# A decoder layer on one core: gate and up rows of the experts dealt to partitions in runs of eight

## The chip, the cores and the metric

The kernel runs on one core of one Trainium2 chip. The metric is device time in microseconds (us), from runs of the whole layer. Engines are named as in the profile: PE is the matmul engine (PEld its weight load), DVE the vector engine, ACT the scalar engine, POOL GpSimd, SP the engine that issues most of the transfers. The transfers of all queues run on 16 DMA engines.

## The reference, cut to what matters

One layer of a decoder with 1024 tokens of 1024 columns: a combined input projection, two kinds of causal attention side by side, an output projection, cross-attention into 256 memory tokens, and a mixture of 32 experts in 4 groups, of which each token takes the best two of its best group. The change is in the last part:

```python
hf = h.reshape(n_tok, d)                       # normalised rows, 1024 x 1024
xb = h_pad[tok]                                # the rows that chose expert e
hidden = jax.nn.silu(xb @ w_gate[e]) * (xb @ w_up[e])     # 1024 x 256 each
y = (hidden @ w_down[e]) * wt[:, None]                     # 256 x 1024
out = zeros.at[slot_token].add(y)
```

`xb @ w_gate[e]` sums over the 1024 columns of a row. In which order, and which 128 of them share a step, is free, as long as the columns of `xb` and the rows of the weights agree.

## The kernel before, in words

All instructions are recorded first, with the tiles that they read and write, and then issued in an order that a list scheduler with a fixed cost model finds (class `Sched`; what it issues has line 481 in the profile). Everything of size is one of 50 tiles of 4 KB per partition.

**Router.** For each tile of 128 tokens, `r_keep(t)` multiplies the rows with the norm's gain on POOL (`xn<-xr,gb`), scales them with each row's factor on ACT, and stores them with SP into the DRAM table `XN`, one row of 4 KB a token. On DVE run the choice of the experts (`r_top`, tiles `rtmp` and `A`), the ranks (`r_rank`) and the factors (`fs`). `r_index` makes the table of row numbers `gidx`, by which the experts gather.

**Experts.** `experts()` goes over the 32 experts. For each, `moe_piece` loads six pieces of 512 KB into tiles `eraw`: pieces 0 to 3 hold 256 rows each of gate and of up (two DMAs of 256 KB), pieces 4 and 5 hold 128 rows each of down (one DMA of 512 KB). `m_split` makes of each piece two parts that the matmul takes exactly: `ehi` (a copy on ACT) and `elo` (a subtraction on DVE). `m_x` gathers up to 96 token rows from `XN` (POOL, `xg<-XN,gidx`) and transposes them, 128 columns at a time, into `xT`. `m_gu` multiplies: for each of 8 blocks of 128 columns three matmuls (high by high, high by low, low by high) into one PSUM bank whose first 256 columns are gate and last 256 up. `m_h` and `m_d` transpose the product and multiply with down; POOL adds the rows into `ACC` with an indirect DMA. The first four experts multiply with the down weights as they are (`WHOLE_D`); no expert does so with gate and up (`WHOLE_GU` is empty).

In `moe_piece`, piece j of gate takes the weight rows 256j to 256j + 255; partition p gets rows 256j + p and 256j + 128 + p. So each partition gets two runs of 1 KB from gate and two from up. The transposed block k of a token row holds columns 128k to 128k + 127.

A last part (from line 1828 on) handles experts with more than 96 tokens, if there are any. In the profiled execution its body is not entered.

Of the kernel before, what the change touches and what calls it, by code (L numbers as in the profile page):

```python
# [22 lines left out]
P = 128  # L23
D = 1024
S = 1024
KT = D // P
# [53 lines left out]
# Instructions are recorded with the tiles they read and write, and issued in the order in which  # L80
# a list scheduler with a simple cost model starts them.
# [6 lines left out]
def _sizes(side, kw, shape=None):  # L88
    """The axes of one side of a rearrange pattern, as lists of names."""
    out, group = [], None  # L90
    for tok in side.replace("(", " ( ").replace(")", " ) ").split():
        if tok == "(":
            group = []
        elif tok == ")":
            out.append(group)
            group = None
        elif group is None:
            out.append([tok])
        else:
            group.append(tok)  # L100
    return out


class View:
    """A part of a lazily allocated tile."""
# [58 lines left out]
class LazyTile:  # L164
    def __init__(self, pool, shape, dtype, kw, slot):
        self.pool, self.shape, self.dtype, self.kw, self.slot = pool, tuple(shape), dtype, kw, slot
        self.real, self.log, self.left, self.end = None, [], 0, 0
        self.seq, self.strict, self.reserve = slot["count"], False, slot["reserve"]
        self.cap = pool.sched.caps.get(kw["name"])
        slot["count"] += 1  # L170
        # a PSUM bank is taken only once all that is to be written there by the tensor engine can be
        self.whole, self.wait, self.at = pool.psum and kw["name"] != "acc", 0, 0
# [29 lines left out]
class Sched:  # L202
    def __init__(self, nc):
        self.nc, self.ops = nc, []
        self.free = dict.fromkeys(("tensor", "vector", "scalar", "gpsimd", "sync"), 0)
        self.dma_free, self.table = 0, 0
        # for tiles of some names, the places that they share
        self.caps = {n: [0] * c for n, c in dict(CAPS, bank=NB_S, acc=NB_A, lbank=NB_L).items()}
        self.window, self.busy, self.warm = 0, 0, False
        for e in self.free:  # L210
            setattr(self, e, Engine(self, e))
# [7 lines left out]
    def cost(eng, name, a, k, out, views):  # L219
        """Nanoseconds on the engine, and until the result is there."""  # L220
# [27 lines left out]
    def either(self, *ways):  # L248
        """Records an instruction, or a few of one engine; several ways: the scheduler chooses one."""
# [22 lines left out]
        for v in views:  # L272
# [3 lines left out]
            # the tensor engine's writes to a bank stay in order  # L276
# [3 lines left out]
            for o, b, ow in t.log:  # L280
                # the engines take turns at a bank, whatever they do there
# [11 lines left out]
    @staticmethod  # L293
    def hold(*views):
        """Instructions recorded after the next flush use these tiles too."""
        for v in views:
            v.tile.left += 1
# [6 lines left out]
    def flush(self):  # L304
# [17 lines left out]
        queue = {e: [] for e in self.free}     # (time ready, idx, op)  # L322
        avail = {e: [] for e in self.free}     # (idx, op)
# [6 lines left out]
        while done < len(ops):  # L330
            best = None
            for e in self.free:
# [4 lines left out]
                # the first one whose tiles have room  # L337
# [55 lines left out]
    def seen(op, eng):  # L393
        """When an engine can go on from an instruction."""
# [6 lines left out]
    def room(self, op):  # L401
        """When the tiles that the instruction is the first to use can be had; None: not known yet."""
# [16 lines left out]
        for slot, n, before, reserve in need.values():  # L419
            # some places are for the tiles that come before in program order  # L420
# [38 lines left out]
    def clock(self, now, cost):  # L459
        """The tensor engine's clock is halved after a window in which it was little busy."""  # L460
# [55 lines left out]
def hybrid_kernel(ctx: ExitStack, tc: tile.TileContext, a, out):  # L516
# [28 lines left out]
    # everything of size is a tile of 4 KB per partition  # L545
# [8 lines left out]
    def carve(name):  # L554
        """Small tensors as parts of such a tile."""
# [77 lines left out]
    def rsqrt(dst, v, tmp):  # L633
        """dst = 1 / sqrt(v): a first guess from the bits, and three steps of Newton's."""
# [7 lines left out]
    def rsqrt_mean(dst, ss, n, tmp):  # L642
        """dst = 1 / sqrt(ss / n + eps); ss is lost."""
# [3 lines left out]
    def two(name):  # L647
        """Two parts of a [128, 512] operand."""
        return t4(name, P, 2, CH, dt=F32R)
# [13 lines left out]
    def split(dst, src, g=None, eng="vector"):  # L663
        """src (times g) as the sum of two parts that the tensor engine takes exactly."""
# [7 lines left out]
    class Weights:  # L672
        """Column blocks of weights, loaded ahead of their use, in parts [rows, 128 of them, columns]."""
# [16 lines left out]
        def get(self, i):  # L690
            """A function from the row block to its two parts."""
# [12 lines left out]
    def weave(*lists):  # L704
        """Calls the units of all lists, each list's spread evenly over all or a part of the time."""
# [8 lines left out]
    # =================== projections ===================  # L714
# [26 lines left out]
    def x_first(t):  # L741
        """The same for one tile, so that the first products need not wait for a chunk."""
# [20 lines left out]
    # low-rank queries, keys and the rotary key, token-major  # L763
# [22 lines left out]
    # angles of the rotary part  # L786
# [4 lines left out]
    def reduce_angle(ang, tmp):  # L791
        """ang modulo 2 pi, within [-pi, pi] but for rounding"""
# [10 lines left out]
    def c_angles():  # L803
# [6 lines left out]
        # feature-major tables: even heads' has the rotary rows last, odd heads' first; the other rows scale only  # L810
# [32 lines left out]
    def out_split(po, dsts, g=None):  # L843
        """Two parts of a PSUM bank, stored; dsts: where to, and from which partitions."""
# [5 lines left out]
    # rotary key, four copies side by side  # L850
# [25 lines left out]
    # differential queries and keys  # L876
# [15 lines left out]
    # latent queries: columns of a head as [no position | rotary | rotary, halves swapped],  # L892
    # odd heads with the first part last
# [39 lines left out]
    def v_out(po, n0, nh, dst, t):  # L933
        """Values of nh heads from n0 on as [high | low] (even heads) and [low | high]."""
# [36 lines left out]
    # =================== attention ===================  # L971
# [12 lines left out]
    def make_dist(i):  # L984
        """-|pos_q - pos_k| / scale, and far below zero above the diagonal"""
# [81 lines left out]
    def item(kind, h, c):  # L1067
        """Units of one head and half of its queries: the softmaxes, the products with the values."""
# [73 lines left out]
    def attention(items):  # L1142
        """All units of some items: an item's softmaxes along with the products of the one before."""
# [7 lines left out]
    # =================== output projection, memory, router ===================  # L1151
# [8 lines left out]
    # memory's keys and values  # L1160
# [47 lines left out]
    # output norms: one factor for each token and head  # L1208
# [70 lines left out]
    def factors(c, tiles, name):  # L1279
        """1 / rms of the rows of some tiles, in two steps."""  # L1280
# [10 lines left out]
    def cross_units(c):  # L1291
        """The rows of a chunk, transposed, times the gain and in two parts; their factors are for later."""
# [12 lines left out]
    # cross-attention  # L1305
# [78 lines left out]
    # router  # L1384
# [26 lines left out]
    def r_T(t, kk):  # L1411
        """Half a tile's columns, transposed and in two parts."""
# [19 lines left out]
    def r_keep(t):  # L1432
        """The tile's normalised rows, kept in DRAM for the experts."""
        x = t4("xn")
        nc.gpsimd.tensor_mul(x, xr[t], rt["gb"])
# [4 lines left out]
    def r_factors(c, *sizes):  # L1440
        """Units of the rows' factors, and of the tiles' transposes, logits and rows."""
# [16 lines left out]
    def first_max(v, m, oh, cm, wcol):  # L1458
        """One-hot of the first largest along the last axis, and the largest, step by step."""
# [16 lines left out]
    def r_top(c):  # L1476
        """The chunk's choices of experts."""
# [20 lines left out]
    def r_weights(c, take, gl, gm, goh, m12):  # L1498
# [15 lines left out]
        # in three exact parts  # L1514
# [13 lines left out]
    def r_rank(c):  # L1528
        """Rank of each choice among its expert's."""
# [25 lines left out]
    def r_index():  # L1555
        """The table of the first NS choices of every expert."""
# [15 lines left out]
    def r_slots():  # L1572
        """The weights of the table's choices."""
# [15 lines left out]
    def r_over():  # L1589
        """Blocks beyond an expert's first: how many, and where they start."""  # L1590
# [17 lines left out]
    # =================== experts ===================  # L1608
# [12 lines left out]
    def moe_piece(e, j):  # L1621
        """Of an expert's six pieces: two row blocks of gate and up each, or a row block of down."""
# [3 lines left out]
        if j < 4:  # L1626
            for w, o in ((w_g, 0), (w_u, 256)):
                nc.sync.dma_start(raw[:, :, o:o + 256], w[e, j * 256:(j + 1) * 256].rearrange("(k p) f -> p k f", p=P))
        else:
            nc.sync.dma_start(raw.rearrange("p a c -> p (a c)"), w_d[e, (j - 4) * P:(j - 3) * P])  # L1630

# [12 lines left out]
    def m_x(e):  # L1644
        """Gathers the expert's tokens and transposes them."""
# [19 lines left out]
    def m_gu(e):  # L1665
        gu = bank()
        for k in range(KT):
            x = st[e]["x"][k // 4]
            sl = slice((k % 4) * NS, (k % 4 + 1) * NS)
            if e in WHOLE_GU:  # L1670
                mm(gu[0:NS], x[:, sl], pieces[e, k // 2][:, k % 2], start=k == 0, stop=k == KT - 1)
            else:
                wh, wl = st[e][k // 2]
                mm3(gu[0:NS], x[:, 0, sl], x[:, 1, sl], wh[:, k % 2], wl[:, k % 2], k == 0, k == KT - 1)
# [52 lines left out]
    # =================== the order of it all ===================  # L1727
# [21 lines left out]
    # units of work on a common time line, which gives the priorities  # L1749
# [9 lines left out]
    def place(units, *knots):  # L1759
        """Spreads units over the stretches between knots, as many on each."""  # L1760
# [57 lines left out]
    # choices beyond an expert's first NS, in blocks of one expert each  # L1818
# [10 lines left out]
    with tc.If(rnov > 0):  # L1829
# [30 lines left out]
        # a choice that is among the first NS matches no lane  # L1860
# [40 lines left out]
        with tc.For_i(0, rnov, 1) as b:  # L1901
# [7 lines left out]
            for i in range(4):  # L1909
                for src, o in ((w_g, 0), (w_u, 256)):  # L1910
                    nc.sync.dma_start(wgu[i][:, :, o:o + 256], src[bass.ds(ev, 1), i * 256:(i + 1) * 256].rearrange(
                        "o (k p) f -> p (o k) f", p=P))
# [36 lines left out]
    # =================== end: sum and norm ===================  # L1949
# [40 lines left out]
```

## Time and profile before

| | |
|---|---|
| median of 3 runs | 1263.01 us (1262.37 to 1264.27) |
| the profiled execution, first to last instruction | 1263.7 us (no other time of that execution is given) |
| PE busy | 1119.0 us, 89% |
| DVE busy | 903.8 us, 72% |
| ACT busy | 803.1 us, 64% |
| POOL busy | 423.3 us, 33% |
| DMA packets | 177883, 256.56 MB, of them 131058 under 2 KB |

The page shows one execution. Its first part gives each engine's busy time, the second cuts the span into 40 slices of 31.6 us and gives the busy share of each engine and of the DMA engines in tenths. A busy share says where an engine works, not what ends the wait of another; for that there are the chain of waits (the work that ended last, followed back) and the list of who waited for whom. A DMA share over 100% in a short stretch means that an engine works on more than one packet at a time.

### The profile page before, as it was taken

How to read it: one execution, taken by the hardware profiler on the slowest of the kernel's cores; microseconds unless marked ns; L12 is line 12 of the kernel's file. 1: busy time of each engine (PE TensorE's matmuls, PEld its weight loads, DVE VectorE, ACT ScalarE, POOL GpSimd, SP SyncE). 2: the span in 40 equal slices, each digit the busy share in tenths (PEclk: the TensorE clock that was granted, in tenths of full speed). 3: DMA queues.
4: the chain of work that ended last, by engine and by line, in shares of the span. 5: the costliest groups of instructions: out<-in, count | busy, mean ns of one | idle time of the engine just before them, and what ended most of it. 6: DMA issues, size and time to landing. Idle time of an engine off the chain costs nothing.

```text
span 1263.7 us, 19612 instructions
## 1 busy us (share of the span) xinstructions
PE 1119.0 (89%) x6285; PEld 915.9 (72%) x6285; DVE 903.8 (72%) x2100; ACT 803.1 (64%) x1597; POOL 423.3 (33%) x370
## 2 busy tenths in 40 slices
PE   4999999998888998888999999995999988888970
PEld 3988888896767876677899888874666656566640
DVE  5846525478799889988573467786678877777855
ACT  5744326679786778777371455632677877777862
POOL 2214311278554555746411001233133322221110
PEclk8999999997898999788999999995999999999995
DMA  9039897359636462445531132766899999999977
GB/s 291 18 106 314 316 356 223 110 169 265 155 96 146 123 162 62 114 121 194 173 122 47 34 103 70 284 233 232 251 293 275 299 291 311 307 316 315 334 218 272
DMA packets 177883, 256.56 MB, mean 203 GB/s; under 512 B 17035, under 2 KB 131058, under 8 KB 177778
## 3 DMA queue, kind: packets, MB, share of 16 engines
q1 hardware_dynamic: 161728, 208.22, 53.0%
q0 software_dynamic: 15680, 46.75, 12.2%
q8 instruction: 50, 0.82, 0.3%
q14 instruction: 55, 0.45, 0.1%
q10 hardware_dynamic: 370, 0.32, 0.1%
HBM read 208.57 MB, written 55.05 MB: 209 GB/s over the span
## 4 chain that ended last, share of the span: by engine, by line
PE 49%; DMA 24%; DVE 15%; ACT 6%; issue 4%; POOL 1%; SPq 0%; ACTq 0%; DVEq 0%; POOLq 0%
PE lbank L481 29%; DMA eraw<-in_w_expert_up_dram 16%; PE bank L481 15%; PE acc L481 5%; DMA eraw<-in_w_expert_down_dram 4%; DVE mx L481 4%; DVE pT L481 1%; ACT pt L481 1%; DVE pt L481 1%; DMA eraw<-in_w_expert_gate_dram 1%; DVE ss L481 1%; ACT pT L481 1%; DMA ACC<-y,gidx 1%; DVE yt L481 1%; DVE wlo L481 1%
## 5 line engine op out<-in xcount | busy, mean ns | idle before, releaser
L481 DVE TENSOR_TENSOR elo<-eraw,ehi 128x1024 fp32r<-128x1024 f32 x184 | 221.6, 1222 | 54.5 <-ACT ehi L481 50.7
L481 ACT CAST ehi<-eraw 128x1024 fp32r<-128x1024 f32 x184 | 189.6, 1050 | 38.8 <-DMA eraw<-in_w_expert_up_dram 28.5
L481 PE MATMUL bank<-ehi,xT 128*96 128x512 f32 x512 | 175.3, 414 | 16.8 <-ACT y L481 15.6
L481 PE MATMUL bank<-k,q 128*128 128x512 f32 (+5 forms) x480 | 137.6, 393 | 21.7 <-ACT pt L481 9.8
L481 DVE TENSOR_TENSOR pT<-bank,pT 128x512 fp32r<-128x512 f32 (+1 forms) x208 | 109.3, 560 | 31.6 <-ACT pT L481 31.2
L481 PEld LDWEIGHTS bank<-ehi,xT 128*96 128x96 f32 x512 | 86.4, 169 | 56.3 <-ACT y L481 19.3
L481 POOL DMA_INDIRECT ACC<-y,gidx x32 | 53.2, 1664 | 216.2 <-ACT y L481 150.3
L481 PE MATMUL acc<-pT,v 128*128 128x512 f32 (+3 forms) x384 | 116.3, 389 | 9.3 <-ACT pT L481 4.7
L481 PE MATMUL bank<-hc,pt 128*128 128x128 f32 x640 | 109.7, 301 | 8.8 <-POOL pt L481 3.2
L481 PEld LDWEIGHTS bank<-k,q 128*128 128x128 f32 (+1 forms) x480 | 87.1, 205 | 41.5 <-ACT pt L481 13.1
L481 ACT CAST pT<-bank 128x512 fp32r<-128x512 f32 (+1 forms) x208 | 93.2, 495 | 28.9 <-PE bank L481 27.7
L481 PE MATMUL bank<-elo,xT 128*96 128x512 f32 x256 | 105.3, 411 | 4.8 <-DVE elo L481 4.7
L481 PEld LDWEIGHTS bank<-hc,pt 128*128 128x128 f32 x640 | 86.6, 156 | 21.3 <-ACT pt L481 4.2
L481 PE MATMUL lbank<-whi,mix 128*128 128x256 f32 x512 | 96.6, 285 | 0.0
L481 PE MATMUL lbank<-whi,hT 128*128 128x256 f32 (+1 forms) x384 | 86.2, 312 | 0.0
L481 PEld LDWEIGHTS acc<-pT,v 128*128 128x128 f32 x384 | 67.5, 202 | 24.8 <-DVE pT L481 9.2
L481 PE MATMUL lbank<-hT,whi 128*128 128x512 f32 x256 | 81.6, 395 | 0.0
L481 PEld LDWEIGHTS lbank<-whi,mix 128*128 128x128 f32 x512 | 81.1, 191 | 0.1
L481 PE MATMUL bank<-ehi,hid 128*96 128x512 f32 x224 | 75.4, 395 | 1.8 <-DVE xT L481 1.0
L481 ACT ACTIVATE pt<-bank,mx 128x512 f32<-128x512 f32 (+2 forms) x96 | 55.3, 581 | 30.4 <-DVE mx L481 26.9
L481 DVE TENSOR_REDUCE mx<-bank 128x1 f32<-128x512 f32 (+3 forms) x112 | 61.2, 567 | 16.0 <-PE bank L481 15.8
L481 PE MATMUL lbank<-wlo,mix 128*128 128x256 f32 x256 | 72.4, 283 | 0.0
(622 smaller groups left out, 2703.9 us busy)
## 6 DMA issues: line engine op xcount, KB each, us to landing
eraw<-in_w_expert_gate_dram SPq DMA_DIRECT2D x128, 256.0 KB
eraw<-in_w_expert_up_dram SPq DMA_DIRECT2D x128, 256.0 KB
eraw<-in_w_expert_down_dram SPq DMA_DIRECT2D x64, 512.0 KB
k<-KD SPq DMA_DIRECT2D x72, 128.0 KB
QM<-st POOLq DMA_DIRECT2D x16, 512.0 KB, 5.3
q<-QM SPq DMA_DIRECT2D x16, 512.0 KB
wraw<-in_w_out_dram SPq DMA_DIRECT2D x16, 512.0 KB
wraw<-in_w_in_dram SPq DMA_DIRECT2D x12, 512.0 KB
```

Source lines behind the costliest of these rows:

```text
L481: getattr(getattr(self.nc, eng), name)(*[real(v) for v in a], **{n: real(v) for n, v in k.items()})
```

## The change

The weight rows of gate and up are dealt out in runs of eight: partition p now gets rows 8p to 8p + 7 of each matrix. Piece j holds of these the rows 8p + 2j and 8p + 2j + 1, which lie behind each other in DRAM: one run of 2 KB per partition and DMA, in place of two of 1 KB. A piece's tile now has gate in its first half and up in its second, with two rows in each; `gate_up` picks from it, for the matmul, one row of gate and one of up: two runs of 256 columns which lie 512 columns apart, where there was one run of 512.

So that the transposed block k holds the columns 8q + k, `r_keep` stores a token's row with its columns in that order: column 8q + k goes to place 128k + q. The multiplication on POOL reads its operands in order and writes each float 128 floats away from the one before.

```diff
     def r_keep(t):
         x = t4("xn")
-        nc.gpsimd.tensor_mul(x, xr[t], rt["gb"])
+        nc.gpsimd.tensor_mul(x.rearrange("p (k q) -> p q k", k=KT), *[
+            v.rearrange("p (q k) -> p q k", k=KT) for v in (xr[t], rt["gb"])])
         nc.scalar.activation(x, x, AF.Copy, scale=rs_[t])
...
         if j < 4:
-            for w, o in ((w_g, 0), (w_u, 256)):
-                nc.sync.dma_start(raw[:, :, o:o + 256], w[e, j * 256:(j + 1) * 256].rearrange("(k p) f -> p k f", p=P))
+            for i, w in enumerate((w_g, w_u)):
+                nc.sync.dma_start(raw[:, i], w[e].rearrange("(p k) f -> p (k f)", k=KT)[:, j * 512:(j + 1) * 512])
...
+    def gate_up(v, kk):
+        return v.rearrange("p i (k f) -> p k i f", k=2)[:, kk]
...
                 wh, wl = st[e][k // 2]
-                mm3(gu[0:NS], x[:, 0, sl], x[:, 1, sl], wh[:, k % 2], wl[:, k % 2], k == 0, k == KT - 1)
+                mm3(gu[0:NS], x[:, 0, sl], x[:, 1, sl], gate_up(wh, k % 2), gate_up(wl, k % 2), k == 0, k == KT - 1)
```

The part for further blocks of an expert reads its gate and up weights in the same order of rows; it is not entered here. Comments and docstrings were also taken out.

No instruction moves: on all five engines the same instructions stand in the same order with the same waits. What differs is the shape of 256 loads on SP (128 x 2 x 256 before, 128 x 512 after) and of 8 products on POOL (128 x 1024 before, 128 x 128 x 8 after), and the operand that 768 matmuls of `m_gu` read.

## Rows read from the trace of the kernel before

**Rows 1.** Page, part 2: mean busy share of the DMA engines in 40 slices.

```profile
DMA  9039897359636462445531132766899999999977
```

**Rows 2.** Busy time by stretch: us from and to, length, engines, clock, DMA share, GB/s.

```profile
core 0: us, PE busy (x) PEld busy (x) DVE busy (x) ACT busy (x) POOL busy (x), PEclk, DMA share, GB/s
883.00:930.00 47.00, 46.34 (x199) 29.24 (x198) 30.63 (x36) 31.57 (x48) 9.81 (x8) 0.95 0.85 258
930.00:1215.00 285.00, 256.69 (x1196) 176.30 (x1195) 224.13 (x257) 220.53 (x311) 72.41 (x49) 0.97 1.01 306
```

**Rows 3.** Chain of waits, 930 to 1215 us: shares of that stretch by engine and line.

```profile
by line: DMA eraw<-in_w_expert_up_dram 68.9%; DMA eraw<-in_w_expert_down_dram 17.1%; DMA eraw<-in_w_expert_gate_dram 3.1%; ACT ehi L481 2.2%; PE bank L481 2.1%; DVE elo L481 2.0%; issue 1.9%; SPq L481 1.4%; ACT y L481 0.7%; ACT sg L481 0.3%
```

**Rows 4.** What SP waited for, 930 to 1215 us: total us, times, longest.

```profile
SPq L481 <- DMA eraw<-in_w_expert_up_dram: 51.4, 65, 3.5
...
SPq L481 <- PE bank L481: 14.5, 16, 1.6
```

**Rows 5.** DMA, 930 to 1215 us: packets by size, and the queue of SP's loads.

```profile
DMA packets 63897, 87.34 MB, mean 306 GB/s; under 512 B 6149, under 2 KB 54780, under 8 KB 63875
...
q1 hardware_dynamic: 58335, 74.09, 81.1%
```

**Rows 6.** SP's issues: the loads in the stretches of rows 9 and 10.

```profile
338.49 0.54 SPq L481 DMA_DIRECT2D q<-QM  x1
...
803.99 1.07 SPq L481 DMA_DIRECT2D wraw<-in_w_mem_o_dram  x2
```

**Rows 7.** SP's queue, 846.5 to 850.5 us: gate and up, 1 KB packets alone.

```profile
q1 hardware_dynamic: 1468, 1.42, 109.2%
```

**Rows 8.** SP's queue, 613 to 615 us: `w_mem_q` and `w_out`, 1 KB packets alone.

```profile
q1 hardware_dynamic: 754, 0.76, 108.5%
```

**Rows 9.** SP's queue, 808 to 810 us: `w_mem_o`, 2 KB packets alone.

```profile
q1 hardware_dynamic: 372, 0.76, 101.7%
```

**Rows 10.** SP's queue, 340 to 341 us (`q<-QM`), then 342 to 345 (`k<-KN`): 2 KB packets.

```profile
q1 hardware_dynamic: 176, 0.36, 97.6%
...
q1 hardware_dynamic: 358, 0.66, 100.9%
```

**Rows 11.** SP's queue, 1242 to 1247 us: rows of `ACC`, 4 KB packets alone.

```profile
q1 hardware_dynamic: 554, 2.03, 103.8%
```

**Rows 12.** Timeline of POOL: start, us, instruction, idle before.

```profile
804.21 2.37 POOL L481 TENSOR_TENSOR wlo<-wraw,whi 128x1024 fp32r<-128x1024 f32 x1 [6.99 <-ACT whi L481]
825.63 2.41 POOL L481 TENSOR_TENSOR xn<-xr,gb 128x1024 f32<-128x1024 f32 x1 [19.05 <-DVE xr L481]
...
850.56 3.29 POOL L481 TENSOR_TENSOR xn<-xr,gb 128x1024 f32<-128x1024 f32 x1 [9.60 <-DVE rper L481]
...
875.61 1.08 POOL L481 DMA_INDIRECT xg<-XN,gidx  x1 [3.68 <-issue]
```

**Rows 13.** Timeline of DVE, 825 to 842 us.

```profile
825.66 2.52 DVE L481 TENSOR_TENSOR A<-rtmp 128x128 bf16<-128x128 f32 x1
...
830.91 0.28 DVE L481 TENSOR_TENSOR A<-rtmp 128x128 bf16<-128x128 f32 x1
```

**Rows 14.** POOL's groups by shape: count, busy us, mean ns, idle before.

```profile
L481 POOL TENSOR_TENSOR rtmp<-A,hc 128x256 bf16<-128x256 bf16 x4 | 2.4, 616 | 10.3 <-issue 8.7 <-DVE A L481 1.5
...
L481 POOL TENSOR_TENSOR wr<-wr,gcol 128x288 f32<-128x288 f32 x1 | 1.2, 1177 | 47.0 <-PE lbank L481 47.0
```

**Rows 15.** Timeline of ACT: the last scaling of token rows.

```profile
862.23 1.15 ACT L481 ACTIVATE xn<-xn,fs 128x1024 f32<-128x1024 f32 x1 [5.21 <-issue]
```

**Rows 16.** Timeline of PE, 924 to 928 us: matmuls of `m_gu` behind each other.

```profile
924.09 0.63 PE L481 MATMUL bank<-ehi,xT 128*96 128x512 f32 x2
...
924.79 0.63 PE L481 MATMUL bank<-ehi,xT 128*96 128x512 f32 x2
```

**Rows 17.** Timeline of PE, 588 to 598 us: matmuls of 256 columns behind each other.

```profile
591.07 0.28 PE L481 MATMUL lbank<-whi,mix 128*128 128x256 f32 x1
...
591.55 0.28 PE L481 MATMUL lbank<-wlo,mix 128*128 128x256 f32 x1
```

More of the change, by code (lines that the diff above doesn't have):

```diff
@@ L1670, in m_gu @@
             if e in WHOLE_GU:
-                mm(gu[0:NS], x[:, sl], pieces[e, k // 2][:, k % 2], start=k == 0, stop=k == KT - 1)
+                mm(gu[0:NS], x[:, sl], gate_up(pieces[e, k // 2], k % 2), start=k == 0, stop=k == KT - 1)
             else:
                 wh, wl = st[e][k // 2]
-                mm3(gu[0:NS], x[:, 0, sl], x[:, 1, sl], wh[:, k % 2], wl[:, k % 2], k == 0, k == KT - 1)
+                mm3(gu[0:NS], x[:, 0, sl], x[:, 1, sl], gate_up(wh, k % 2), gate_up(wl, k % 2), k == 0, k == KT - 1)
         sg = t4("sg")[:, 0:FF]
@@ L1910, in hybrid_kernel @@
                 for src, o in ((w_g, 0), (w_u, 256)):
-                    nc.sync.dma_start(wgu[i][:, :, o:o + 256], src[bass.ds(ev, 1), i * 256:(i + 1) * 256].rearrange(
-                        "o (k p) f -> p (o k) f", p=P))
+                    nc.sync.dma_start(wgu[i][:, :, o:o + 256], src[bass.ds(ev, 1)].rearrange(
+                        "o (p k) f -> p (o k) f", k=KT)[:, 2 * i:2 * i + 2])
             for i in range(2):
```

## The prediction, made before the changed kernel ran

> **What bounds the kernel now.** I read the 40 slices first: from about 880 us to 1200 us the DMA engines stand at 9 tenths or more [rows 1]. The stretches then split the experts in two [rows 2]. From 883 to 930 us PE is busy for 46.3 of 47 us while the loads run at 258 GB/s: there PE works off what was loaded ahead. From 930 to 1215 us the DMA share is 1.01, and PE is busy for 256.7 of 285 us, DVE for 224, ACT for 221. The chain of waits of that stretch lies to 89.1% in loads of weights (68.9, 17.1 and 3.1) [rows 3]; that gate stands so low only means that up is issued behind it and lands last. SP does not hold the loads back: it waits mostly for an earlier load to land (51.4 us for up), and only 14.5 us for PE to free a tile [rows 4]. So 285 us of the run are bound by how long the DMA engines take for the packets, and the other engines leave room: if the loads took no time, PE's 256.7 us would be left. The page gives the span, 1263.7 us, and nothing around it; the median of the runs is 0.7 us lower.
>
> **Shorter packet time for gate and up.** Packets between 512 B and 2 KB in the bound stretch: 54780 less 6149, so 48631 of 1 KB [rows 5], all of them gate or up. They become 24316 packets of 2 KB. What does a packet take? I divide share times length times 16 engines by the number of packets (bytes over packet size, since the counts hold small ones too), in stretches that hold one size alone, known by SP's issues just before them [rows 6]. Gate and up at 1 KB: 109.2% x 4 us x 16 / 1387 = 50.4 ns [rows 7]. Other weights at 1 KB: 108.5% x 2 x 16 / 742 = 46.8 ns [rows 8]. 2 KB packets into 128 partitions: 101.7% x 2 x 16 / 371 = 87.7 ns for `w_mem_o` [rows 9], and 97.6% x 16 / 176 = 88.7 ns for `q<-QM` [rows 10]. 4 KB: 103.8% x 5 x 16 / 496 = 167 ns [rows 11]. So a pair of 1 KB packets takes 100.8 ns and its successor 88.7 (I take the longer): 12.1 ns saved x 24316 / 16 engines = 18.4 us of DMA time.
>
> Bounds: if the pair is set at the best 1 KB packets, 93.6 ns, the saving is 4.9 ns or 7.4 us. If rates are compared instead of packet times, gate and up ran at 355 GB/s (1.42 MB in 4 us), the best 1 KB stretch at 380 (0.76 in 2), 2 KB at 380 too: against 355 that is 6.6% of 49.8 MB / 355 GB/s = 140 us, 9.2 us; against 380 it is nothing. From above, the bound stretch itself: the queue's 81.1% x 285 x 16 = 3698 us, less 5930 packets of 4 KB (its 74.09 MB less 49.80) at 167 ns, leaves 55.7 ns per 1 KB packet; 111.4 less 88.7 is 22.7 ns a pair, 34.5 us, of which at most 28.3 can be had before PE's 256.7 us bind. The shares above 1.05 say that engines overlap small packets, so packet time overstates a gain, and the rate understates it, since in the bound stretch the share is 1.01 and not 1.09. I take the middle of 9.2 and 18.4: 13.8 us; ends 0 and 28. Of it 89.1% passes on, the part of the chain that lies in loads: 12.3 us. What is late next is PE, 256.7 us of then about 273, and the splits on ACT and DVE; that is the cover that keeps me from passing on more.
>
> [...]
>
> The other packets of gate and up (65536 in all, by 64 MB of weights) are loaded ahead, before 930 us, and there PE is the bound [rows 2]: I cost them at nothing.
>
> **The store order of the token rows.** Eight products on POOL, 2.4 us each [rows 12], now write floats 512 B apart. This is not a matter of POOL alone. The DVE instruction that makes `A` takes 0.28 us at 830.91, but 2.52 us at 825.66, and then ends 0.1 us after the POOL product that began at 825.63 [rows 12, 13]: DVE stood still until POOL was done. It is one of three such places in the router, within 13 us, where behind the stalled instruction the rest of the choice, the ranks and at last the gathers queue on DVE. So each ns that a product gets longer is paid three times. The other five are covered: four run before POOL idles for 7 us, which ends at 804.21; the last ends at 853.9, and ACT takes its result at 862.23 [rows 12, 15], 8.4 us later. What the stride costs no row shows. From below: 0, and POOL's products whose operands are cut in small pieces (`rtmp`, 616 ns for 256, 2.4 ns each) run as fast as whole ones (2410 / 1024 = 2.4) [rows 12, 14]. From above: the slowest product of size, `wr`, takes 1177 / 288 = 4.1 ns an element, which would make 4.2 us of 2.4: +1.8 x 3 = 5.4 us. I take +0.4 each, nearer to `rtmp`, 1.2 us in all.
>
> [...]
>
> **The matmul's operand in two runs.** 24 matmuls per expert, 626 in the stretch, read two runs of 256 columns. Behind each other they go every 0.233 us (924.09 to 924.79 for three) [rows 16]. Matmuls of 256 columns go every 0.12 us (591.07 to 591.55 for four) [rows 17], so even two starts would cost 0.240, 4.4 us of PE in the stretch, under the loads. I take 0.
>
> **Sum.** 1263.7 - 12.3 + 1.2 = 1252.6 us for the profiled execution, 0.7 less for the median: 1251.9, say 1252. With 7 to 18 us saved on DMA and 0 to 3.6 paid on the router this case runs from 1247 to 1260.
>
> **Rivals.**
>
> 1. *The bytes bind, not the packets.* For it: 380 GB/s with 1 KB packets and with 2 KB [rows 8, 9]. Against it: 2.03 MB in 5 us at 4 KB, 406 GB/s [rows 11]. Then gate and up gain 0 to 2 us and the router loses 1: 1262 to 1263. [...] Chance 0.2. A load that the chip cuts to 1 KB all the same, so that the change doesn't do what it says, would give this time too.
>
> 2. *The full packet time comes back.* The bound stretch's own 55.7 ns, 28 us saved, PE as the bound: 1263.7 - 0.891 x 28 + 1.2 - 0.7 = 1239. For it: the share of 1.01 shows no idle DMA engine. Against it: ACT and DVE are each busy for 221 to 224 us, with waits for each other between. Chance 0.13.
>
> 3. *The stores on POOL cost more than the loads save.* A float at a time, 512 B apart, slows a product so far that DVE stands three times for longer. It decides from 12.3 / 3 = 4.1 us more per product, so 6.5 us in place of 2.4. At four times the time (9.6 us) the three stalls give 21.6 us: 1263.0 - 12.3 + 21.6 = 1272. For it: no row shows a scattered write, and the stalls are there. Against it: `rtmp`'s cut operands cost nothing. Chance 0.1.
>
> 4. *Each load touches the same quarter of every 8 KB,* and its packets wait for each other in DRAM. 2 KB packets do come slow in this trace: `k<-KN` into 64 partitions, 100.9% x 3 x 16 / 322 = 150 ns [rows 10]. That is 49 ns a pair more, 75 us, 1338; it decides from 100.8 ns a packet. Against it: `q<-QM`, whose partitions are 8 KB apart too, takes 88.7 ns [rows 10]. Chance 0.05.
>
> **How the numbers follow.** The forecast has 0.52, the rivals 0.2, 0.13, 0.1 and 0.05. Within 0.2% (2.5 us, about what a measurement of this kernel tells from no change) lie the first rival, less a seventh, and a little of the forecast and of POOL's rival: same 0.19. Faster: 0.5 of the forecast, 0.13, and the rest of the first rival: 0.66. Slower: 0.15, rivals 3 and 4. The range of 8 in 10 goes from 1242, between the forecast and the second rival, to 1265, past the first.
>
> **What would show it.** In the profile after: some 33 thousand packets fewer on SP's queue; between 930 us and the end of the loads the same bytes in some 273 us, at 318 to 322 GB/s; the chain there still in loads, with a larger part on PE; PE's matmuls of `m_gu` every 0.233 us; POOL's products under 3 us, and DVE's instruction beside the first of them under 3.2. I am wrong about the loads if the GB/s stay near 306, about the reserve of PE if they rise without the end moving, and about the router if the first gather comes more than 4 us later than at 875.6 us [rows 12].

## The result, and the profile after

| | before | after | ratio |
|---|---|---|---|
| median, first comparison (5 and 5 runs) | 1264.27 us (1262.37 to 1266.15) | 1257.39 us (1255.11 to 1257.89) | 0.9936 [0.992, 0.9953] |
| median, second comparison (15 and 10 runs) | 1264.55 us (1261.4 to 1266.55) | 1258.08 us (1256.37 to 1263.63) | 0.9962 [0.9946, 0.9978] |
| profiled execution | 1263.7 us | 1255.6 us | |

By the medians the change makes the kernel 6.9 and 6.5 us faster, by the ratios 8 and 5 us, where 11 us were forecast. The direction, the place and the mechanism were right; a cost that the sum did not have took 3 to 5 us back.

The times in the last line run from the first to the last instruction. A run's time is 1.8 us more (1257.39 us for the profiled execution after), so the one before took about 1265.5 us, near the upper end of its runs, and the 8.1 us between the two profiles overstate the gain by some 1 us.

The page of the changed kernel, its third part: packets in all, then SP's queue with packets, MB and share of 16 engines.

```profile
DMA packets 145115, 256.56 MB, mean 204 GB/s; under 512 B 17035, under 2 KB 65522, under 8 KB 145010
...
q1 hardware_dynamic: 128960, 208.22, 52.8%
```

There are 32768 packets fewer, half of the 65536 of gate and up, and not a byte less. Now the same two stretches as in [rows 2]; the second ends where the last load has landed, at 1206.0 us. Columns as there.

```profile
883.00:930.00 47.00, 47.00 (x205) 29.54 (x206) 30.32 (x36) 31.74 (x48) 9.80 (x8) 0.97 0.85 267
930.00:1207.00 277.00, 256.54 (x1193) 176.57 (x1192) 222.82 (x257) 218.76 (x310) 73.98 (x49) 0.97 0.98 314
```

The bound stretch is 277 us long instead of 285, at 314 GB/s instead of 306, with the same 256.5 us of PE in it. All that the run gained, it gained here. The DMA share has fallen from 1.01 to 0.98. The DMA view of that stretch answers to [rows 5]:

```profile
DMA packets 39470, 87.10 MB, mean 314 GB/s; under 512 B 6137, under 2 KB 6137, under 8 KB 39448
...
q1 hardware_dynamic: 33953, 74.01, 78.2%
```

No 1 KB packets are left. By the queue's packets and bytes some 5962 are of 4 KB (24.42 MB) and 24214 of 2 KB (49.59 MB). The queue's 78.2% x 277 x 16 = 3466 us, less 5962 x 167 ns, leaves 102.0 ns per 2 KB packet, where the pair of 1 KB packets took 111.4 by the same working. The traces also hold each packet's own duration: on this queue a 1 KB packet took 52.7 ns before (930 to 1215 us), so 105.5 a pair, and a 2 KB packet takes 96.8 ns after. The working by the share puts both too high, mainly because the 4 KB packets took 185 and 182 ns in these stretches and not 167.

The chain of waits of that stretch, by line, answers to [rows 3], and SP's waits between 930 and 1207 us (us in total, times, longest) to [rows 4]:

```profile
by line: DMA eraw<-in_w_expert_up_dram 65.3%; DMA eraw<-in_w_expert_down_dram 17.2%; issue 8.2%; DMA xg<-XN,gidx 3.6%; DMA ACC<-y,gidx 3.4%; POOL xg L481 0.8%; POOL ACC L481 0.7%; ACT ehi L481 0.4%; ACT y L481 0.2%; SPq L481 0.1%; ACT hid L
```

```profile
SPq L481 <- DMA eraw<-in_w_expert_gate_dram: 63.6, 84, 3.2
SPq L481 <- DMA eraw<-in_w_expert_up_dram: 55.9, 82, 3.0
SPq L481 <- DMA eraw<-in_w_expert_down_dram: 54.2, 44, 3.3
...
SPq L481 <- PE bank L481: 3.5, 8, 1.8
```

Loads still end last: 82.5% of the chain, and another 7% lies in gathers and adds, which are transfers too. From 977 us on the chain is almost only loads; before that it runs through POOL's gathers and adds, and most of the 8.2% "issue", time in which the profile shows nothing that was waited for, lies there. PE, of which the prediction expected a larger part, is not among the lines shown. SP waits for PE even less than before (3.5 us against 14.5). So the DMA engines bind after the change as before it.

The router. POOL's timeline (start, us, idle before) and DVE's answer to [rows 12] and [rows 13]; the third fence is POOL's group of all eight products, before and after, with the mean in ns behind the busy time.

```profile
826.86 2.41 POOL L481 TENSOR_TENSOR xn<-xr,gb 128x1024 f32<-128x1024 f32 x1 [19.00 <-DVE xr L481]
...
874.79 1.08 POOL L481 DMA_INDIRECT xg<-XN,gidx  x1 [3.68 <-issue]
```

```profile
826.89 2.52 DVE L481 TENSOR_TENSOR A<-rtmp 128x128 bf16<-128x128 f32 x1
...
832.15 0.28 DVE L481 TENSOR_TENSOR A<-rtmp 128x128 bf16<-128x128 f32 x1
```

```profile
L481 POOL TENSOR_TENSOR xn<-xr,gb 128x1024 f32<-128x1024 f32 x8 | 20.1, 2512 | 56.3 <-issue 23.7 <-DVE xr L481 19.9 <-DVE rper L481 9.6
...
L481 POOL TENSOR_TENSOR xn<-xr,gb 128x1024 f32<-128x1024 f32 x8 | 19.3, 2412 | 54.9 <-issue 23.7 <-DVE xr L481 19.9 <-DVE rper L481 8.3
```

The scattered store costs nothing: a product takes 2.41 us. Before, the median of the eight was 2.40 us; the mean is 2.51 because one took 3.29 [rows 12]. DVE's stall beside the first product in the fence is 2.52 us as before. The gathers begin at 874.79 us, not later than before.

PE's timeline answers to [rows 16]:

```profile
923.24 0.62 PE L481 MATMUL bank<-ehi,xT 128*96 128x512 f32 x2
...
923.93 0.63 PE L481 MATMUL bank<-ehi,xT 128*96 128x512 f32 x2
```

Three matmuls in 0.69 us, one every 0.23: reading the operand as two runs costs nothing either.

### The profile page after: what moved, and what is told of

Its sections match the earlier page's. It is cut to its first block, busy times and chain, and to the rows that moved or that the text cites. A ratio compares the mean times of both kernels' runs of the same rounds, so it can differ in the third digit from the quotient of the medians.

```text
span 1255.6 us, 19611 instructions
## 1 busy us (share of the span) xinstructions
PE 1112.2 (89%) x6285; PEld 910.8 (73%) x6285; DVE 904.1 (72%) x2100; ACT 800.6 (64%) x1597; POOL 424.9 (34%) x370
## 3 DMA queue, kind: packets, MB, share of 16 engines
q0 software_dynamic: 15680, 46.75, 12.4%
## 5 line engine op out<-in xcount | busy, mean ns | idle before, releaser
L481 PE MATMUL lbank<-whi,mix 128*128 128x256 f32 x512 | 96.6, 285 | 0.0
```

The lines of the kernel that those rows point to most:

```text
L481: getattr(getattr(self.nc, eng), name)(*[real(v) for v in a], **{n: real(v) for n, v in k.items()})
```

## The experiments

Ratios are to the kernel before on the same chip: its median was 1264.27 us beside experiments 1 to 4, 1266.08 beside 5 and 6, and 1264.55 beside the four kernels of experiment 7. The diffs show the loads alone, not what follows from them (the columns' order in the stored rows, the operands of the matmuls).

**1. The order of rows alone (e1_deal_1k).** The changed kernel, but each partition's two neighbouring rows land behind each other in separate packets of 1 KB; the matmul's operand is one run again, and the store on POOL stays scattered.

```diff
-            for i, w in enumerate((w_g, w_u)):
-                nc.sync.dma_start(raw[:, i], w[e].rearrange("(p k) f -> p (k f)", k=KT)[:, j * 512:(j + 1) * 512])
+            for w, o in ((w_g, 0), (w_u, 256)):
+                nc.sync.dma_start(raw[:, :, o:o + 256], w[e].rearrange("(p k) f -> p k f", k=KT)[:, 2 * j:2 * j + 2])
```

> The rows of gate and up are dealt in runs of eight and the stored columns follow, as in the change, but each 2 KB run lands as two runs of 1 KB, so packets are 1 KB as before and the matmul reads one run of 512 columns again. Packet size (theory): the gain is gone, 1262 to 1266 us, 306 GB/s in the bound stretch. Order of rows in DRAM (rival): the gain stays, 1255 to 1259 us. If the split operand of the matmul or the scattered store cost something, this run also shows it: below 1262 only with packets unchanged.

Measured: 1267.25 us (12 runs) against 1264.27 (17 runs), ratio 1.0017 [1.0001, 1.0032]. That is a little above the range of the theory. The new order and the scattered store are still there and the gain is gone; so it goes with the size of the packets (the matmul's operand went back too, but it cost PE nothing in the change). The new order of rows by itself costs, if anything, 0.17%. POOL's products are not the reason: they take 2527 ns here, and 2512 before, both with one slow one of 3.3 us among the eight. The stretch from 930 to 1190 us ran at 302 GB/s in the profiled execution, the slowest of the twelve, where the kernel before had 304 (experiment 7):

```profile
930.00:1190.00 260.00, 234.61 (x1089) 161.41 (x1088) 199.03 (x231) 197.04 (x280) 70.28 (x47) 0.96 1.00 302
```

**2. The packets alone (e2_pairs_2k).** 2 KB packets, but each load reads 256 neighbouring rows, two per partition, so that partitions lie 2 KB apart in DRAM and not 8 KB. The token rows' columns are stored to match.

```diff
-                nc.sync.dma_start(raw[:, i], w[e].rearrange("(p k) f -> p (k f)", k=KT)[:, j * 512:(j + 1) * 512])
+                nc.sync.dma_start(raw[:, i], w[e, j * 256:(j + 1) * 256].rearrange("(p k) f -> p (k f)", k=2))
```

> Packets of 2 KB as in the change, but partition p of piece j takes rows 256j + 2p and 256j + 2p + 1, so that one load reads 256 KB in one piece instead of 2 KB out of every 8 KB. Packet size alone (theory): as the change, 1255 to 1259 us. Rival, that the 8 KB pitch costs something and ate part of the gain: 2 KB packets fall from a mean of 97 ns in the bound stretch towards 88, 24212 x 9 / 16 = 13.6 us of packet time, of which about half comes through: 1249 to 1252 us.

Measured: 1254.18 us (1251.39 to 1256.18), ratio 0.9912 [0.9892, 0.9932]: 3.2 us better than the change, with intervals that still touch, and between the two expectations. It was the first sign that the order of rows has a price of its own; experiment 7 settles it.

**3. Packets of 4 KB (e3_gu_4k).** One load of 512 KB takes four rows per partition of one matrix, and the gate's matmuls (256 columns) come before up's. PE has twice as many matmuls for gate and up, half as wide.

```diff
-            for i, w in enumerate((w_g, w_u)):
-                nc.sync.dma_start(raw[:, i], w[e].rearrange("(p k) f -> p (k f)", k=KT)[:, j * 512:(j + 1) * 512])
+            nc.sync.dma_start(raw.rearrange("p a c -> p (a c)"), (w_g, w_u)[j // 2][e].rearrange(
+                "(p k) f -> p (k f)", k=KT)[:, (j % 2) * 1024:(j % 2 + 1) * 1024])
```

> Packets of 4 KB for gate and up: a piece is four rows of one matrix per partition (one load of 512 KB), and gate and up get matmuls of 256 columns, one after the other; the result is the same. If the loads still bind the experts after the change (theory): 49.8 MB at 406 in place of 380 GB/s, 8 us less, nine tenths of it coming through, 1249 to 1252 us. If PE, the splits and the waits between them hold the loads back by now (rival), nothing comes through, and PE's 4 us more cost up to that: 1256 to 1262 us.

Measured: 1246.24 us (1244.94 to 1247.24), ratio 0.9849 [0.9826, 0.9871]. That is 3 us under the range of the theory. Larger packets go on to pay, so what bound the changed kernel was still the loads; how much of the gain is the size of the packets, experiment 5 tells.

**4. The loads alone (e4_rates).** Nothing but loads of gate and up, in five shapes one after the other and then all again; the output is a copy of the input. One execution.

> Loads alone, no computing: 24 MB each of gate and up in five layouts, twice over: 1 KB packets as before, 2 KB as in the change (8 KB pitch), 2 KB in pairs (2 KB pitch), 1 KB with the rows of the change, 4 KB. The output is a copy of the input x, not the layer. By rates (theory: engines overlap small packets, so the packet's own time overstates its cost): 1 KB 355 to 380 GB/s at a share of 1.09, 2 KB 380, 4 KB 406, so 2 KB gains up to 7%. By packet times (rival): 1 KB packets 50 ns, 2 KB 88 ns, and the GB/s rise by the same 14%. If the pitch matters, 2 KB at 8 KB pitch is below 2 KB in pairs.

The DMA view, one stretch within each shape: all packets with their rate, then SP's queue (packets, MB, share). In turn: 1 KB as before; 2 KB as in the change (partitions 8 KB apart); 2 KB in neighbouring rows; 1 KB in the change's order; 4 KB. The last two pairs are the second round of the two 2 KB shapes.

```profile
DMA packets 21683, 20.91 MB, mean 349 GB/s; under 512 B 1275, under 2 KB 21682, under 8 KB 21682
q1 hardware_dynamic: 21682, 20.90, 110.3%
...
DMA packets 10572, 19.25 MB, mean 385 GB/s; under 512 B 1174, under 2 KB 1174, under 8 KB 10572
q1 hardware_dynamic: 10572, 19.25, 105.5%
...
DMA packets 11686, 21.29 MB, mean 387 GB/s; under 512 B 1298, under 2 KB 1298, under 8 KB 11685
q1 hardware_dynamic: 11685, 21.28, 105.5%
...
DMA packets 20794, 20.05 MB, mean 346 GB/s; under 512 B 1223, under 2 KB 20793, under 8 KB 20793
q1 hardware_dynamic: 20793, 20.04, 109.1%
...
DMA packets 5613, 20.44 MB, mean 409 GB/s; under 512 B 623, under 2 KB 623, under 8 KB 5613
q1 hardware_dynamic: 5613, 20.44, 102.5%
...
DMA packets 10518, 19.16 MB, mean 383 GB/s; under 512 B 1167, under 2 KB 1167, under 8 KB 10517
q1 hardware_dynamic: 10517, 19.15, 104.6%
...
DMA packets 10620, 19.35 MB, mean 387 GB/s; under 512 B 1176, under 2 KB 1176, under 8 KB 10620
q1 hardware_dynamic: 10620, 19.35, 105.5%
```

Alone, the rate goes 349, 385, 409 GB/s from 1 KB to 2 KB to 4 KB: bytes do not bind at 1 KB. The 10 to 11% from 1 KB to 2 KB lie between the theory's 7% and the rival's 14%. The share goes 110, 105, 102%: the smaller the packets, the more the engines overlap them, so a sum over packet times makes small packets look worse than they are. The packets' own durations overstate in the same way: 102.4 ns for a pair of 1 KB packets and 88.6 for one of 2 KB would make 16%, and the rate rose by 10 to 11%. The rows' order alone costs little here: 385 and 383 against 387 at 2 KB, 346 against 349 at 1 KB, 0.5 to 1% each time and in the same direction.

**5. The same order of instructions, with packets of 2 KB (e5_gu4_pairs, e6_gu4_2x2k).** The 4 KB kernel changes the size of a load and the order of matmuls too. Both are kept here, with 2 KB packets instead: in e5 a load takes two blocks of 256 neighbouring rows, in e6 two loads of 256 KB take rows 8 KB apart. The lines are against experiment 3.

```diff
-                "(p k) f -> p (k f)", k=KT)[:, (j % 2) * 1024:(j % 2 + 1) * 1024])
+                "(b p k) f -> p b (k f)", p=P, k=2)[:, (j % 2) * 2:(j % 2 + 1) * 2])        # e5
+            for i in range(2):                                                              # e6
+                nc.sync.dma_start(raw[:, i], src[:, i * 512:(i + 1) * 512])
```

> As the run with 4 KB packets (512 KB loads of one matrix, gate's matmuls before up's, the same order of all instructions), but each partition's 4 KB come as two runs of 2 KB from places 256 KB apart in DRAM. If the packets make the difference (theory), the gain from 1254 (2 KB pairs) to 1246 us is gone and this run takes 1252 to 1256 us. If the larger loads and the order of gate before up make it (rival), it takes 1245 to 1249 us.

> As the run with 4 KB packets, but each piece comes as two loads of 256 KB with 2 KB packets at the change's 8 KB pitch. Packets (theory): 1254 to 1259 us, like the change. Larger loads (rival 1, what counts is 512 KB per load): 1254 to 1259 here while the 512 KB load with 2 KB packets stays near 1246. Gate before up (rival 2): 1245 to 1249 us here too.

Measured: e5 1251.59 us (1247.27 to 1256.95), ratio 0.9894 [0.9868, 0.992]; e6 1255.07 us (1252.26 to 1257.81), ratio 0.9911 [0.9892, 0.9931]. Against experiment 3, on the same chip, packets of 4 KB are worth another 5 us at the same order of instructions, with intervals that just touch; so 5 of the 11 us that experiment 3 gains on the change go to the size of the packets alone, though the runs of e5 scatter by 10 us. The rest can lie in the order of rows, the larger loads or gate before up; no pair of runs here parts them. Rows 8 KB apart are again the slower of the 2 KB shapes, by 3.5 us, but the intervals overlap, and e6 has twice as many loads as well.

**6. Where PE would bind (e7_noacc_before, e8_noacc_after).** Both kernels without the 32 indirect DMAs that add the experts' rows into `ACC`, so that the other traffic is smaller.

```diff
-        nc.gpsimd.indirect_dma_start(out=ACC[:, :], out_offset=Rows(ap=gidx[0:NS, e:e + 1], axis=0), in_=y[0:NS],
-                                     in_offset=None, bounds_check=S - 1, oob_is_err=False, compute_op=OP.add)
```

> The kernel before without the 32 indirect DMAs that add the experts' rows into ACC, so the output lacks the experts' part. They take about 2700 packets of 4 KB at 327 ns, some 50 us of DMA time in the bound stretch. If the loads bind it (theory), the loads end 25 us or more earlier, 1225 to 1238 us, at which PE binds. If something else holds the experts (rival), 1255 us or more.

> The changed kernel without the same 32 indirect DMAs; the output lacks the experts' part. If PE and the splits have a floor of their own well under 1257 us and the loads bind above it (theory), this run ends within 5 us of the run of the kernel before without them, near the floor, 1222 to 1235 us. If after the change other engines already held the experts at 1257 us (rival), it stays above 1250 us.

Measured: 1221.37 us (0.9651 [0.9628, 0.9675]) from the kernel before, 1215.53 us (0.9594 [0.957, 0.9618]) from the changed one. One stretch of each, first the kernel before and then the changed one (length, PE, PEld, DVE, ACT, POOL, clock, DMA share, GB/s):

```profile
1000.00:1100.00 100.00, 98.10 (x479) 69.62 (x478) 89.73 (x105) 85.91 (x124) 12.25 (x10) 1.00 1.05 306
```

```profile
1000.00:1100.00 100.00, 99.13 (x486) 70.37 (x485) 90.54 (x105) 87.84 (x129) 13.86 (x11) 1.00 1.02 343
```

Without the adds PE is busy nearly all the time, and the layer ends at 1221 and 1215 us, a little under both ranges that were expected. That is far below 1257: neither PE nor the splits on DVE and ACT keep the changed kernel from going faster. The adds cost the kernel before 45 us and the changed one 42, but not by their traffic alone. Part of it lies behind the experts. In the kernel before, the rows of `ACC` are read back behind the last add, 8.3 us after PE's last matmul has ended; in e7 the reads are issued 11.6 us ahead of that end (two pieces of the chain of before, then a line of SP's timeline of e7):

```profile
1231.32 5.22 DMA ACC<-y,gidx
...
1236.68 3.27 DMA yt<-ACC
```

```profile
1181.18 4.38 SPq L481 DMA_DIRECT2D yt<-ACC  x8
```

PE's last matmul itself ends 35.6 us earlier in e7, at 1192.8 in place of 1228.4 us, and the other 11 us of the 46.9 between these two executions come after it. The expectation's 2700 packets were too many, since they hold the gathers: between 880 and 1215 us POOL's queue has 3846 packets of 4 KB with the adds and 1914 without. The last weights are issued at 1172.75 us in e7 and at 1160.31 in e8, 12.4 us apart, of which only 2.0 reach the end of these two executions (1216.8 and 1214.8 us) and 5.8 the medians: there PE has become the bound.

**7. The order of rows, side by side (e9_after_again, e10_pairs_again, e11_gu_4k_again, e12_gu_4k_quads).** The change, experiment 2 and experiment 3 once more, and a fourth kernel: 4 KB packets whose load reads 512 neighbouring rows, so that partitions lie 4 KB apart and not 8.

```diff
-            nc.sync.dma_start(raw.rearrange("p a c -> p (a c)"), (w_g, w_u)[j // 2][e].rearrange(
-                "(p k) f -> p (k f)", k=KT)[:, (j % 2) * 1024:(j % 2 + 1) * 1024])
+            nc.sync.dma_start(raw.rearrange("p a c -> p (a c)"), (w_g, w_u)[j // 2][
+                e, (j % 2) * 512:(j % 2 + 1) * 512].rearrange("(p k) f -> p (k f)", k=4))
```

> The changed kernel once more, as the measure for the three runs beside it. Every theory expects 1255 to 1259 us, ratio to the kernel before 0.992 to 0.995.

> 2 KB packets, but each load reads 256 neighbouring rows, so partitions lie 2 KB apart and not 8 KB. Theory pitch (partitions 8 KB apart make a 2 KB packet dearer by some 2 ns under the kernel's full traffic): 0.2 to 0.3% faster than the changed kernel of the same chip, some 3 us, ratio 0.990 to 0.992. Theory size (the size of a packet alone counts, the earlier difference of 3 us was chance): the same as the changed kernel within 0.1%.

> 4 KB packets, loads of 512 KB of one matrix, partitions 8 KB apart. Theory size: 1245 to 1248 us, 0.7 to 1.0% under the changed kernel of the same chip. Theory chance (the first run of it was lucky): within 0.4% of the changed kernel.

> 4 KB packets as in the run before it, but each load reads 512 neighbouring rows, so partitions lie 4 KB apart and the load is one run of 512 KB. Theory pitch: 2 to 4 us under the run with 8 KB, so 1242 to 1245 us. Theory size: the same as that run within 0.1%.

Measured: the change 1258.08 us (1256.37 to 1263.63), as expected, ratio 0.9962 [0.9946, 0.9978], a little above; neighbouring pairs 1252.94 us (1249.28 to 1256.14), ratio 0.9911 [0.989, 0.9932]; 4 KB packets 8 KB apart 1245.96 us, ratio 0.9857 [0.9838, 0.9877]; 4 KB packets 4 KB apart 1246.84 us, ratio 0.9864 [0.9841, 0.9886]. At 2 KB the order costs 5.1 us, more than the 3 us of the theory, and the two sets of runs do not overlap. At 4 KB no cost is seen, against the theory's 2 to 4 us; the intervals leave room for 2 to 3 us, and PE, busy for 95% there, may hide a part. The theory of the pitch holds at 2 KB alone.

The same 260 us, 930 to 1190, in the kernel before, the change (e9), the pairs (e10) and the 4 KB packets (e11):

```profile
930.00:1190.00 260.00, 233.79 (x1101) 162.06 (x1100) 203.10 (x234) 200.67 (x283) 69.03 (x47) 0.97 1.00 304
```

```profile
930.00:1190.00 260.00, 240.56 (x1136) 166.69 (x1134) 209.49 (x243) 206.88 (x294) 76.67 (x48) 0.97 0.99 315
```

```profile
930.00:1190.00 260.00, 243.31 (x1138) 167.78 (x1137) 209.26 (x244) 205.55 (x297) 72.20 (x48) 0.97 0.99 317
```

```profile
930.00:1190.00 260.00, 246.63 (x1771) 217.08 (x1770) 216.53 (x253) 211.88 (x303) 69.37 (x49) 0.98 0.98 329
```

The rate at which the stretch is fed, last number, puts these executions in the order of their spans: 304, 315, 317, 329 GB/s and 1263.7, 1254.8, 1254.3, 1245.5 us. The traces of the change and of the pairs are of executions only 0.5 us apart, the pairs' being the slowest of its six; so the 5.1 us stand on the runs' times and not on these two lines. PE's busy time goes up beside it, to 95% in the last one; its cover is nearly used up there.

The 4 KB kernel of experiment 3 beats both kernels, by 1.4 to 1.5% and 0.9 to 1.0%.

## Why the prediction was right, and where its size was off

**What binds.** Right. The whole gain lies between 930 us and the landing of the last load, loads end last after the change too, and the loads alone run faster with larger packets (experiment 4). The stretch shrank less than forecast: 277 us at 314 GB/s in place of 273 at 318 to 322. Taking other traffic away leaves 1215 us (experiment 6), so the reserve that the prediction gave PE is real.

**The packet time, 13.8 us.** Right in size, in part by luck: it is the middle of two workings, 9.2 and 18.4, and no row gave it. By the prediction's working 111.4 - 102.0 = 9.4 ns x 24214 / 16 = 14.2 us of packet time are gone, by the packets' own durations 8.7 ns, 13.2 us. But of these only 8.0 us left the stretch, some 60% and not the 89.1% that the prediction passed on. Part of the rest may be the overlap: the packet time of the whole stretch fell from 1.01 x 285 to 0.98 x 277, by 16 us, and the stretch by 8. The share does not tell whether the other half was time in which an engine worked on two packets at once or is idle time now. Experiment 4 shows the overlap with nothing else running: with 1 KB packets the share is 110.3%, with 2 KB packets 105.5%. The prediction saw that packet time overstates and rates understate, and took the middle; then it multiplied by the chain's share. The rate's 9.2 us x 0.891 = 8.2 would have been right for this kernel, though for the wrong reason, as the next point shows. The upper bound took 55.7 ns for a 1 KB packet of the bound stretch; it was 52.7, mainly since the 4 KB packets beside it took 185 ns and not 167.

**The step that failed: the order of rows at no cost.** The sum had no term for partitions 8 KB apart. The prediction had it only as its fourth rival, all or nothing, 75 us at a chance of 0.05, and argued against it by `q<-QM`, whose 2 KB packets at the same distance take 88.7 ns [rows 10]. That row was read in 1 us without other traffic. In experiment 7 the distance costs 5.1 us, in the first comparison 3.2, in experiment 5 3.5, and in experiment 1 with 1 KB packets perhaps 2; only experiment 7 is clear of the scatter. Without it 2 KB packets gain 10.1 and 11.6 us (experiments 2 and 7), which is the 12.3 of the forecast but for 1 or 2 us. So the account by the medians is: 10 to 11.6 gained by the size of the packets, 3 to 5 lost to the order of rows, 6.5 to 6.9 left.

What makes the distance dear is open. The mean of a 2 KB packet between 930 and 1150 us is 98.0 and 97.2 ns in the two traces of the change, 95.7 and 96.6 ns in the two of the pairs. That is 0.6 to 2.3 ns, times 24214 / 16 = 0.9 to 3.5 us: some or most of the loss, but not surely all. In experiment 5 the two means are 96.9 and 97.1 ns, though the two profiled executions are 10.5 us apart, so packet time alone does not make these differences. No run here shows the DRAM itself. At 8 KB the runs here show 0.5 to 1% of the rate with loads alone (383 and 385 against 387 GB/s, experiment 4).

**The store of the token rows, +1.2 us.** Wrong in size, and small: the products take 2412 ns, the stall 2.52 us, and no cost is seen. The lower end of its bounds was right, and `rtmp` with its cut operands was the row to go by. The 3.6 us that the range has as the router's upper end are shown by no run; what the runs showed is a median product of 2412 ns against 2403 before, and a first gather at 874.79 us against 875.61.

**The matmul's operand, 0.** Right: one matmul every 0.23 us, and experiment 1, with the operand in one run, is no faster.

**The rivals.** The first (bytes bind) falls by experiment 4. The second (28 us come back) falls by the 8 us measured. PE, which it took as the next bound, was not reached: the loads could still go faster, as 1246 us with 4 KB packets shows. The third (POOL) falls by the trace of after. The fourth was right that distance costs and wrong by a factor of 15 to 23 in its price.

## What to carry to other kernels

Where the DMA engines bind, a gain from larger packets is to be read from rates, with the packet times as an upper end, since the engines overlap small packets and that overlap goes with them (experiment 4: a share of 110.3% with 1 KB packets and 105.5% with 2 KB; packet times would make 16%, the rate rose by 10 to 11%). When rows are dealt out anew to make packets larger, first try the deal in which a whole load still reads one piece of DRAM: it gave the 2 KB packets here for 3 to 5 us less. And look one size on: from the better 2 KB shapes to 4 KB it was worth another 5 to 8 us.

## What the runs showed of the hardware that was not expected

- Loads of one core alone reach 349 GB/s with 1 KB packets (346 in the change's order), 383 to 387 with 2 KB, 409 with 4 KB, at DMA shares of 110, 105 and 102%.
- Loads of 2 KB packets that start 8 KB apart cost 3 to 5 us of the layer's 1258 under its full traffic, and 0.5 to 1% of the rate alone; with 4 KB packets no such cost was seen (1245.96 against 1246.84 us).
- A product on POOL that writes each float 512 B from the last takes 2412 ns for 1024 a partition, as one that writes them in a row (median 2403).
- The 32 indirect adds, 96 rows of 4 KB at most each, cost the layer 42 to 45 us, some 11 of them behind PE's last matmul; without them PE is busy for 98 to 99% of the time from 1000 to 1100 us. Most of their 4 KB packets take about 327 ns: on POOL's queue 1861 packets took 320 to 339 ns with the adds and 58 without.
